# One-hots of four tokens in one comparison, and second-table products one tile behind, in a one-core hybrid layer

## The chip, the cores and the metric

The kernel runs on one core of one Trainium2 chip. The metric is the device time of one execution in microseconds; the median of the runs counts. A separate execution is recorded by the hardware profiler, and all rows below come from that one.

## What is computed

The reference is one layer on x (1024 tokens of 1024 numbers): a token mixer (stick-breaking attention and a gated delta rule), a cross-attention into 256 memory tokens, and a product-key retrieval over 16384 single-neuron experts, each added to x, then a final RMSNorm. What the change touches most is the retrieval:

```python
q = (xt @ w_pq).reshape(T, PEER_HEADS, 2, PEER_QDIM // 2)
s = jnp.einsum('thpd,hpnd->thpn', q, subkeys)
top_s, top_i = lax.top_k(s, PEER_TOPK)
...
best_s, best_pos = lax.top_k(cand_s.reshape(T, PEER_HEADS, kk), PEER_TOPK)
expert = jnp.take_along_axis(cand_i.reshape(T, PEER_HEADS, kk), best_pos, axis=-1)
gate = jax.nn.softmax(best_s, axis=-1)
...
act = jax.nn.gelu(jnp.einsum('thkd,td->thk', peer_u[eb], xb), approximate=False) * gb
return jnp.einsum('thk,thkd->td', act, peer_v[eb])
```

Each token picks 128 experts (8 heads of 16) out of 128 x 128. An expert's row of `peer_u` gives a number, Gelu and the gate weigh it, and it multiplies the expert's row of `peer_v`.

## The kernel before

The program is written with tiles and pools. A planner at build time puts the instructions of each engine in an order: it goes through simulated time with its own durations, and where several instructions are ready for an engine it takes the one that the program emits first. On the chip each engine then runs its list in that order, and semaphores hold it where data or a buffer is missing. So the order in which the Python code emits is a priority, not the order on the chip.

The sequence is done in three groups of tokens (256, 384, 384). Each group goes through `token_mixing`, `cross` and `routing`. In `token_mixing`, `proj` loads 128 columns of a weight at a time, splits them into a high and a low half (`split`: ACT rounds, DVE subtracts), and `mm3` makes three products per 128 rows. The loop at line 468 does this for 1536 columns of the delta rule: each result goes into a tile `c` with three columns of the group before in front (line 471, from `tail`), the last three columns are kept for the next group (line 472), then a short convolution follows (one scaled copy on ACT, three steps on DVE). In `cross`, line 636 divides the exponentials of the softmax by their sum, before PE transposes them.

For retrieval the blocks of 128 tokens are served in two ways. Blocks 0, 1, 2, 3 and 7 are fetched: `fetch` on POOL's queue gathers 128 rows of an expert table by index (line 793, 512 KB), and DVE (lines 809 and 83, or PE in line 838) uses them; the tile `row` has seven buffers, also for other uses. Blocks 4, 5 and 6 (384 tokens) are dense: all 16384 experts are computed, in 128 tiles of 128 experts.

For the dense blocks `choose_t` gives `sel3`: for each token's 128 choices the first key, the second key and the gate, one token in a column. `spread` makes a gate table from it: for each token a one-hot of the first key times the gate (`o0`, DVE, line 913) and a one-hot of the second key (`o1`: for even tokens POOL, line 918; for odd ones ACT, as Relu(1 - |n - key|), lines 915 and 916), each 128x128, in twelve buffers. PE multiplies them (line 919), four tokens into one PSUM tile, ACT copies that into `st` (one buffer), and after eight such groups SP stores `st` in `g_sc` (2 MB). There are 96 groups of four tokens.

The first table's products are in `dense_h`: it loads 128 experts' columns of `peer_ut`, splits them, makes 24 products into a PSUM tile and applies Gelu on ACT. `dense_ahead` does this for the first 36 tiles (`AHEAD`) beside the spreading of blocks 5 and 6: `mix` emits one tile, then 1.83 steps of `pick_gates` (33 steps a block), and so on. `dense` does the other 92 tiles and all products with the second table: for each tile `dense_h` (into the single PSUM tile `hp`), then the load of 128 rows of `peer_v` (`vr`, five buffers), their split (`vh`, `vl`, three buffers), the gating of `h` with `gm` (a part of `g_sc`, loaded for four tiles), the split of that (`ah`, `al`), and 18 products into six PSUM tiles that collect over all tiles. The 36 tiles done ahead come last, with `h` loaded from `h_sc`. The dense steps are emitted in turns with `rest`, the fetching of blocks 2, 3 and 7, of which 320 steps are emitted before.

Of the kernel before, what the change touches and what calls it, by code (L numbers as in the profile page):

```python
# [8 lines left out]
F32 = mybir.dt.float32  # L9
# [11 lines left out]
P = 128  # L21
# [12 lines left out]
ROWS = 7  # L34
WLS = 2
SHS = 3
OBS = 12
ND = 384
TMAX = max(n for _, n in GROUPS)
KD = D // P  # L40
# [11 lines left out]
def block_kernel(ctx: ExitStack, tc: tile.TileContext, x_t, mem_t, gains, cst, sel, eye, w_in, conv, a_log,  # L52
# [23 lines left out]
    def copy(o, i, scale=1.0):  # L76
        return act.activation(o, i, AF.Copy, scale=scale)  # L77

    def func(o, i, f, **kw):
        return act.activation(o, i, f, **kw)  # L80
# [28 lines left out]
    def a_tile():  # L109
        return pa.tile([P, 512], F32, name="acc")  # L110
# [4 lines left out]
    def by4(t):  # L115
        return t.rearrange("p (h t) -> p h t", h=4)
# [334 lines left out]
    def token_mixing(g, t0, T, x1_where, result):  # L451
# [3 lines left out]
        with ExitStack() as eo:  # L455
# [12 lines left out]
            for i, ps in proj(w_in, O_G, 1536, xh, xl, T, share=SH_G):  # L468
                c = po.tile([P, T + 3], F32, name="ev", bufs=2)
                copy(c[:, 3:], ps)  # L470
                vec.tensor_copy(c[:, :3], tail[:, i])
                vec.tensor_copy(tail[:, i], c[:, T:])
                d = qkv[i // 4][:, i % 4]
                copy(d, c[:, 0:T], cv[:, i, 0:1])
                for j in range(1, 4):
                    stt(d, c[:, j:j + T], cv[:, i, j:j + 1], d, OP.mult, OP.add)
# [131 lines left out]
    def cross(g, x1, T):  # L608
        NB = T // P
        with ExitStack() as es:  # L610
            p1 = open_pool(f"c1{g}", 1, where=es)
            tmp = open_pool(f"c2{g}", 2, where=es)
            mK = p1.tile([P, KD, NMEM], F32, name="mK")
            sp.dma_start(mK, mk_sc)
            mV = p1.tile([P, 2, D], F32, name="mV")
            sp.dma_start(mV, mv_sc)
            hi, lo = p1.tile([P, KD, T], F32R, name="xhi"), p1.tile([P, KD, T], F32R, name="xlo")
            norm_t(hi, lo, tmp, lambda k: x1[:, k], 1, T)
            qT = p1.tile([P, KD, T], F32, name="qT")
            for i, ps in proj(w_cq, 0, D, hi, lo, T):  # L620
                copy(qT[:, i], ps, 1.0 / 16)
            oh, ol = p1.tile([P, KD, T], F32R, name="xhi"), p1.tile([P, KD, T], F32R, name="xlo")
            for h in range(4):
                pT = tmp.tile([P, 2, T], F32, name="pT")
                for b in range(NB):
                    bs = slice(b * P, (b + 1) * P)
                    s = z_tile()[:, :NMEM]
                    for k in range(2):
                        pe.matmul(s, lhsT=qT[:, 2 * h + k, bs], rhs=mK[:, 2 * h + k], start=k == 0, stop=k == 1)
                    mx = tmp.tile([P, 2], F32, name="mx")  # L630
                    vec.tensor_reduce(mx[:, 0:1], s, op=OP.max, axis=AX.X)
                    vec.tensor_scalar(mx[:, 0:1], mx[:, 0:1], -1.0, None, op0=OP.mult)
                    p = tmp.tile([P, NMEM], F32, name="p")
                    func(p, s, AF.Exp, bias=mx[:, 0:1], accum_out=mx[:, 1:2])
                    vec.reciprocal(mx[:, 1:2], mx[:, 1:2])
                    vec.tensor_scalar(p, p, mx[:, 1:2], None, op0=OP.mult)
                    tp = a_tile().rearrange("p (m t) -> p m t", m=4)[:, :2]
                    for m in range(2):
                        pe.transpose(tp[:, m], p[:, m * P:(m + 1) * P], ident)
                    copy(pT[:, :, bs], tp)  # L640
                for d in range(2):
                    ps = j_tile()[:, :T]
                    for m in range(2):
                        pe.matmul(ps, lhsT=mV[:, m, (2 * h + d) * P:(2 * h + d + 1) * P], rhs=pT[:, m],
                                  start=m == 0, stop=m == 1)
                    split(oh[:, 2 * h + d], ol[:, 2 * h + d], ps)
            for i, ps in proj(w_co, 0, D, oh, ol, T):
                vec.tensor_add(x1[:, i], ps, x1[:, i])
# [251 lines left out]
    def spread(px_, sel3, b):  # L900


        neg = px_.tile([P, 3, P], F32, name="neg")
        vec.tensor_scalar(neg[:, 0], sel3[:, 1], -1.0, None, op0=OP.mult)
        for c0 in range(0, P, 32):
            st = px_.tile([P, P, 32], F32, name="st")
            for c in range(c0, c0 + 32, 4):
                ps = by4(a_tile())
                for j in range(4):
                    o0 = px_.tile([P, P], F32, name="o0", bufs=OBS)  # L910
                    o1 = px_.tile([P, P], F32, name="o1", bufs=OBS)
                    t = c + j
                    vec.tensor_scalar(o0, io128, sel3[:, 0, t:t + 1], sel3[:, 2, t:t + 1], op0=OP.is_equal, op1=OP.mult)
                    if j % 2:
                        func(o1, io128, AF.Abs, bias=neg[:, 0, t:t + 1])
                        func(o1, o1, AF.Relu, scale=-1.0, bias=1.0)
                    else:
                        pool.tensor_scalar(o1, io128, sel3[:, 1, t:t + 1], None, op0=OP.is_equal)
                    pe.matmul(ps[:, j], lhsT=o1, rhs=o0, start=True, stop=True)
                copy(st[:, :, c - c0:c - c0 + 4], ps.rearrange("p j r -> p r j"))  # L920
                yield
            sp.dma_start(g_sc[(b * P + c0) // 32], st)
# [16 lines left out]
    def dense_h(r, xh, xl, ps, o, eng=vec):  # L939

        raw = wp.tile([P, KD, P], F32, name="raw", bufs=3)
        sp.dma_start(raw, ut_v[:, :, r * P:(r + 1) * P])
        uh = wp.tile([P, KD, P], F32R, name="wh")
        ul = wp.tile([P, KD, P], F32R, name="wl", bufs=WLS)
        split(uh, ul, raw, eng=eng)
        mm3(ps, uh, ul, xh, xl, KD)
        func(o, ps, AF.Gelu)
# [11 lines left out]
    def dense(xh, xl):  # L959
        T = ND  # L960
        NB = T // P
        with ExitStack() as es:
            tmp = open_pool("dv", 2, where=es)
            ps = [f() for f in (z_tile, z_tile, z_tile, a_tile, a_tile, j_tile)][:2 * NB]
            hp = j_tile()[:, :T]
            first = True
            for r0 in [*range(AHEAD, P, RG), *range(0, AHEAD, RG)]:
                gm = tmp.tile([P, T // 32, RG, 32], F32, name="gm")
                sp.dma_start(gm, g_sc[:, :, r0:r0 + RG].rearrange("c p r t -> p c r t"))
                h = tmp.tile([P, RG, T], F32, name="h")  # L970
                if r0 < AHEAD:
                    sp.dma_start(h, h_sc[:, r0:r0 + RG, :T])
                for j in range(RG):
                    r = r0 + j
                    if r0 >= AHEAD:
                        dense_h(r, xh, xl, hp, h[:, j])
                    vr = tmp.tile([P, D], F32, name="vr", bufs=5)
                    sp.dma_start(vr, peer_v[r * P:(r + 1) * P])
                    vh = tmp.tile([P, D], F32R, name="vh", bufs=3)
                    vl = tmp.tile([P, D], F32R, name="vl", bufs=3)  # L980
                    split(vh, vl, vr)
                    hj = h[:, j].rearrange("p (c t) -> p c t", t=32)
                    vec.tensor_mul(hj, hj, gm[:, :, j])
                    ah = tmp.tile([P, T], F32R, name="ah", bufs=3)
                    al = tmp.tile([P, T], F32R, name="al", bufs=3)
                    split(ah, al, h[:, j])
                    for b in range(NB):
                        for a, v in ((ah, vh), (ah, vl), (al, vh)):
                            for d in range(2):
                                pe.matmul(ps[2 * b + d], lhsT=a[:, b * P:(b + 1) * P], rhs=v[:, 512 * d:512 * d + 512],  # L990
                                          start=first and a is ah and v is vh, stop=r == (AHEAD or P) - 1 and a is al)
                    first = False
                    yield
            for b in range(NB):
                blk = order[b]
                rows = slice(blk * P, blk * P + P)
                y = tmp.tile([P, D], F32, name="y")
                sp.dma_start(y, xr_sc[rows])
                for d in range(2):
                    dd = slice(512 * d, 512 * d + 512)  # L1000
                    vec.tensor_add(y[:, dd], ps[2 * b + d], y[:, dd])  # L1001
                last_norm(y, rows)
# [135 lines left out]
```

## Time and profile before

| | us |
|---|---|
| median of 3 runs | 3807.42 |
| lowest, highest | 3803.46, 3813.42 |
| the profiled execution, its own time | 3825.46 |
| its span, first to last instruction | 3823.5 |

Over the span PE is busy 3384.8 us (89%), PE's weight loads 2839.4 (74%), DVE 2848.8 (75%), POOL 1982.3 (52%) and ACT 1614.8 (42%); the DMA engines move 1100.54 MB at a mean of 288 GB/s. These shares are means over stages with different limits. The table by stretch shows each stage by itself: the engine that is busy nearly all of a stretch is the candidate for its limit, and the waits say which engine the others waited for at the end. [...] PEclk is the clock that PE was granted, as a part of full speed.

### The profile page before, as it was taken

Reading aid. Unit: us, or ns where it says so; the run is one execution under the profiler, and the core shown is the slowest. Engines: PE = TensorE matmul, PEld = TensorE weight load, DVE = VectorE, ACT = ScalarE, POOL = GpSimd, SP = SyncE. Lnnn points to the kernel's source line nnn. Section 1 sums busy time; section 2 is a strip of 40 time slices with the busy share of each in tenths; the row PEclk is TensorE's granted clock in tenths of the full one; section 3 lists DMA queues with packets and bytes.
Section 4 is the critical chain, followed back from the end, with each engine's and each line's share of the span. In section 5 each row is a group of like instructions: output and inputs, shape, how many; then the busy total and the mean of one; then the engine's idle time right before and its main releaser. Section 6 shows DMA issues by size and latency. Waiting matters only on the chain. (4 is left out here: it accounts for less than half of the span.)

```text
span 3823.5 us, 57005 instructions
## 1 busy us (share of the span) xinstructions
PE 3384.8 (89%) x20621; PEld 2839.4 (74%) x20621; DVE 2848.8 (75%) x5650; ACT 1614.8 (42%) x2982; POOL 1982.3 (52%) x1611
## 2 busy tenths in 40 slices
PE   7998976999889978999987899999659999999995
PEld 6888866887666755757676677888558888888874
DVE  6445599886566799338987568997767888878886
ACT  5654543664323323545533233565533333343333
POOL 1010007767744456467786455778964444444552
PEclk9999988998989988999978999999779999999998
DMA  6537439997898998999869989989899999999996
GB/s 162 141 91 216 146 107 316 342 310 234 310 358 288 334 327 284 302 318 318 271 219 325 328 288 342 302 294 327 300 323 324 340 344 340 338 325 321 358 385 216
DMA packets 745794, 1100.54 MB, mean 288 GB/s; under 512 B 42148, under 2 KB 554532, under 8 KB 742440
## 3 DMA queue, kind: packets, MB, share of 16 engines
q0 software_dynamic: 184320, 671.17, 49.3%
q1 hardware_dynamic: 561192, 425.73, 36.4%
q8 instruction: 162, 2.65, 0.3%
q14 instruction: 120, 0.98, 0.1%
HBM read 1036.60 MB, written 60.16 MB: 287 GB/s over the span
## 5 line engine op out<-in xcount | busy, mean ns | idle before, releaser
L793 POOL DMA_INDIRECT row<-in_peer_u_dram,ix x640 | 821.9, 1284 | 523.3 <-DVE y L83 152.4
L809 DVE CUSTOM_DVE_ANT_0 row<-row,xs 128x1024 f32<-128x1024 f32 x640 | 827.3, 1302 | 149.3 <-DMA row<-in_peer_u_dram,ix 126.1
L223 PE MATMUL pj<-xhi,wh 128*128 128x384 f32 (+1 forms) x1912 | 640.5, 335 | 58.3 <-ACT xhi L77 21.9
L89 DVE TENSOR_TENSOR wl<-raw,wh 128x1024 fp32r<-128x1024 f32 (+1 forms) x420 | 494.9, 1179 | 252.6 <-ACT wh L77 239.3
L223 PE MATMUL pj<-xhi,wl 128*128 128x384 f32 (+1 forms) x1912 | 641.8, 336 | 33.4 <-POOL wl L89 18.0
L223 PE MATMUL pj<-xlo,wh 128*128 128x384 f32 (+1 forms) x1912 | 626.8, 330 | 11.1 <-DVE xlo L89 11.1
L793 POOL DMA_INDIRECT row<-in_peer_v_dram,it x384 | 442.3, 1152 | 364.2 <-PE ac L838 174.3
L77 ACT ACTIVATE wh<-raw 128x1024 fp32r<-128x1024 f32 (+1 forms) x447 | 449.9, 1007 | 276.0 <-PE pj L223 200.6
L793 POOL DMA_INDIRECT row<-in_peer_v_dram,ix x256 | 341.0, 1332 | 372.7 <-DVE y L83 184.2
L223 PEld LDWEIGHTS pj<-xhi,wh 128*128 128x128 f32 x1912 | 375.4, 196 | 90.9 <-ACT xhi L77 28.2
L223 PE MATMUL pj<-xh,wh 128*128 128x384 f32 x1152 | 400.8, 348 | 46.8 <-ACT h L80 40.9
L223 PEld LDWEIGHTS pj<-xhi,wl 128*128 128x128 f32 x1912 | 375.6, 196 | 71.8 <-POOL wl L89 20.1
L223 PE MATMUL pj<-xh,wl 128*128 128x384 f32 x1152 | 399.1, 346 | 9.7 <-POOL wl L89 5.6
L223 PEld LDWEIGHTS pj<-xlo,wh 128*128 128x128 f32 x1912 | 373.3, 196 | 30.8 <-DVE xlo L89 14.8
L223 PE MATMUL pj<-xl,wh 128*128 128x384 f32 x1152 | 394.1, 343 | 0.3 <-DVE xl L89 0.3
L83 DVE SCALAR_TENSOR_TENSOR y<-row,hh,y 128x1024 f32<-128x1024 f32 x256 | 328.3, 1283 | 8.1 <-DMA row<-in_peer_v_dram,ix 6.6
L838 PE MATMUL ac<-row,sb 128*32 128x256 f32 x3072 | 263.0, 402 | 41.9 <-DMA row<-in_peer_v_dram,it 37.8
L89 POOL TENSOR_TENSOR wl<-raw,wh 128x1024 fp32r<-128x1024 f32 x27 | 65.7, 2433 | 427.4 <-DVE one L773 331.4
L223 PEld LDWEIGHTS pj<-xh,wh 128*128 128x128 f32 x1152 | 221.3, 192 | 68.8 <-ACT h L80 55.4
L77 ACT ACTIVATE vh<-vr 128x1024 fp32r<-128x1024 f32 x128 | 134.9, 1058 | 322.0 <-PE pj L990 301.8
L223 PEld LDWEIGHTS pj<-xh,wl 128*128 128x128 f32 x1152 | 221.4, 192 | 24.7 <-POOL wl L89 7.5
L89 DVE TENSOR_TENSOR vl<-vr,vh 128x1024 fp32r<-128x1024 f32 x128 | 156.6, 1223 | 91.1 <-ACT vh L77 80.7
(453 smaller groups left out, 6514.1 us busy)
## 6 DMA issues: line engine op xcount, KB each, us to landing
raw<-in_w_in_dram SPq DMA_DIRECT2D x132, 512.0 KB
raw<-in_peer_ut_dram SPq DMA_DIRECT2D x128, 512.0 KB
vr<-in_peer_v_dram SPq DMA_DIRECT2D x128, 512.0 KB
raw<-in_w_pq_dram SPq DMA_DIRECT2D x48, 512.0 KB
g_sc<-st SPq DMA_DIRECT2D x12, 2048.0 KB
gm<-g_sc SPq DMA_DIRECT2D x32, 768.0 KB
raw<-in_w_mix_dram SPq DMA_DIRECT2D x24, 512.0 KB
raw<-in_w_cq_dram SPq DMA_DIRECT2D x24, 512.0 KB
```

The costliest lines, as they stand in the source:

```text
L77: return act.activation(o, i, AF.Copy, scale=scale)
L83: return vec.scalar_tensor_tensor(out=o, in0=a, scalar=s, in1=b, op0=op0, op1=op1)
L89: eng.tensor_tensor(lo, src, hi, op=OP.subtract)
L223: pe.matmul(ps, lhsT=a[:, k], rhs=b[:, k], start=i == 0, stop=i == 3 * kt - 1)
L793: pool.indirect_dma_start(out=t, out_offset=None, in_=src, in_offset=bass.IndirectOffsetOnAxis(ap=index, axis=0))
L809: vec.tensor_tensor_reduce(out=t, in0=t, in1=xs, scale=1.0, scalar=0.0, op0=OP.mult, op1=OP.add, accum_out=hh[:, j:j + 1])
L838: pe.matmul(ac[32 * d:32 * d + 32, 256 * w:256 * w + 256], lhsT=sb[:, j], rhs=t[:, 256 * d:256 * d + 256], start=j == 0, stop=j == 31)
```

## The change

There are four edits.

- `spread`: for four tokens one DVE instruction compares the numbers 0 to 127 with both keys of each of the four tokens, into a tile `one` (128 x 2 x 4 x 128, three buffers). The one-hot of the first key is multiplied by the gate on ACT, token by token, in place. POOL's comparison, ACT's Abs and Relu, and the negated keys `neg` are gone. The products are the same.
- `dense`: what a tile needs of the second table is a function `weigh`. It is emitted one tile late: first `dense_h` of tile r+1, then `weigh` of tile r. The last one follows the loop.
- `token_mixing`: the two copies of three columns are made by ACT.
- `cross`: the softmax's scaling is made by ACT.

```diff
-OBS = 12
+OBS = 3
...
-                vec.tensor_copy(c[:, :3], tail[:, i])
-                vec.tensor_copy(tail[:, i], c[:, T:])
+                copy(c[:, :3], tail[:, i])
+                copy(tail[:, i], c[:, T:])
...
-                    vec.tensor_scalar(p, p, mx[:, 1:2], None, op0=OP.mult)
+                    copy(p, p, mx[:, 1:2])
...
-        neg = px_.tile([P, 3, P], F32, name="neg")
-        vec.tensor_scalar(neg[:, 0], sel3[:, 1], -1.0, None, op0=OP.mult)
...
+                one = px_.tile([P, 2, 4, P], F32, name="one", bufs=OBS)
+                vec.tensor_tensor(one, io128[:, None, None, :].to_broadcast([P, 2, 4, P]),
+                                  sel3[:, 0:2, c:c + 4, None].to_broadcast([P, 2, 4, P]), op=OP.is_equal)
                 for j in range(4):
-                    o0 = px_.tile([P, P], F32, name="o0", bufs=OBS)
-                    o1 = px_.tile([P, P], F32, name="o1", bufs=OBS)
-                    t = c + j
-                    vec.tensor_scalar(o0, io128, sel3[:, 0, t:t + 1], sel3[:, 2, t:t + 1], op0=OP.is_equal, op1=OP.mult)
-                    if j % 2:
-                        func(o1, io128, AF.Abs, bias=neg[:, 0, t:t + 1])
-                        func(o1, o1, AF.Relu, scale=-1.0, bias=1.0)
-                    else:
-                        pool.tensor_scalar(o1, io128, sel3[:, 1, t:t + 1], None, op0=OP.is_equal)
-                    pe.matmul(ps[:, j], lhsT=o1, rhs=o0, start=True, stop=True)
+                    copy(one[:, 0, j], one[:, 0, j], sel3[:, 2, c + j:c + j + 1])
+                    pe.matmul(ps[:, j], lhsT=one[:, 1, j], rhs=one[:, 0, j], start=True, stop=True)
...
+            def weigh(r, h, gm):
+                vr = tmp.tile([P, D], F32, name="vr", bufs=5)
+                sp.dma_start(vr, peer_v[r * P:(r + 1) * P])
...
+                split(vh, vl, vr)
+                hj = h.rearrange("p (c t) -> p c t", t=32)
+                vec.tensor_mul(hj, hj, gm)
...
+                split(ah, al, h)
...
+            waiting = None
             for r0 in [*range(AHEAD, P, RG), *range(0, AHEAD, RG)]:
...
                 for j in range(RG):
-                    r = r0 + j
                     if r0 >= AHEAD:
-                        dense_h(r, xh, xl, hp, h[:, j])
...
+                        dense_h(r0 + j, xh, xl, hp, h[:, j])
+                    if waiting:
+                        weigh(*waiting)
+                        yield
+                    waiting = r0 + j, h[:, j], gm[:, :, j]
+            weigh(*waiting)
+            yield
```

## Rows read from the trace of the kernel before

**Rows 1.** By stretch: busy us (x instructions) PE, PEld, DVE, ACT, POOL; clock; DMA; GB/s.
```profile
2418.00:2620.00 202.00, 184.61 (x1200) 163.83 (x1199) 191.52 (x619) 132.63 (x312) 173.10 (x160) 0.92 0.87 297
2620.00:2806.00 186.00, 132.82 (x825) 116.94 (x823) 135.85 (x284) 93.91 (x261) 163.03 (x158) 0.82 0.87 302
2722.00:2806.00 84.00, 38.58 (x179) 34.41 (x177) 65.43 (x131) 34.71 (x104) 76.56 (x72) 0.63 0.74 253
...
2838.00:3594.00 756.00, 725.66 (x3596) 647.60 (x3597) 617.06 (x729) 265.45 (x358) 344.79 (x269) 0.99 1.00 337
3500.00:3600.00 100.00, 97.03 (x483) 86.22 (x481) 91.21 (x89) 33.59 (x46) 59.51 (x44) 1.00 1.06 375
```

**Rows 2.** Waits from 2418 to 2806 us: waiter <- releaser, us, times, longest.
```profile
PEld acc L919 <- POOL o L918: 48.7, 25, 8.8
...
PE acc L919 <- POOL o L918: 42.6, 20, 8.6
```

**Rows 3.** The same view from 2840 to 3780 us.
```profile
POOL row L793 <- DVE y L83: 319.5, 154, 23.9
...
PEld pj L223 <- ACT h L80: 40.2, 42, 3.3
...
PE pj L223 <- ACT h L80: 26.8, 42, 3.0
```

**Rows 4.** Timeline of PE: start, duration in us, what.
```profile
3582.18 0.34 PE L223 MATMUL pj<-xl,wh 128*128 128x384 f32 x1
3583.10 0.44 PE L223 MATMUL pj<-xh,wh 128*128 128x384 f32 x1 [0.58 <-ACT h L80]
3583.38 0.34 PE L223 MATMUL pj<-xh,wl 128*128 128x384 f32 x1
3583.55 0.34 PE L223 MATMUL pj<-xl,wh 128*128 128x384 f32 x1
...
3587.37 0.63 PE L990 MATMUL z<-vh,ah 128*128 128x512 f32 x2
...
3591.49 0.34 PE L223 MATMUL pj<-xh,wh 128*128 128x384 f32 x1
```

**Rows 5.** Groups by line and shape, 2400 to 2840 us: busy, mean ns | idle before.
```profile
L918 POOL TENSOR_SCALAR o<-io,sel 128x128 f32<-128x128 f32 x186 | 164.6, 896 | 13.8 <-PE acc L919 11.7
L913 DVE TENSOR_SCALAR o<-io,sel 128x128 f32<-128x128 f32 x372 | 128.6, 414 | 15.4 <-PE acc L919 15.1
...
L80 ACT ACTIVATE o<-io,neg 128x128 f32<-128x128 f32 x186 | 70.2, 396 | 51.5 <-PE acc L919 47.8 <-PE pj L223 3.3
```

**Rows 6.** By stretch, the one-hots (tile o) alone: PE, PEld, DVE, ACT, POOL.
```profile
2418.00:2620.00 202.00, 58.94 (x392) 53.85 (x392) 70.34 (x196) 57.37 (x196) 83.21 (x94) 0.92 0.87 297
2620.00:2806.00 186.00, 66.14 (x376) 59.66 (x376) 58.22 (x176) 51.03 (x176) 81.36 (x93) 0.82 0.87 302
```

**Rows 7.** Groups of ACT and DVE over the whole run, by shape.
```profile
L77 ACT ACTIVATE vh<-vr 128x1024 fp32r<-128x1024 f32 x128 | 134.9, 1058 | 322.0 <-PE pj L990 301.8 <-DMA raw<-in_peer_ut_dram 20.2
...
L80 ACT ACTIVATE h<-pj 128x384 f32<-128x384 f32 x128 | 62.8, 490 | 235.4 <-PE pj L223 223.2 <-issue 12.1
...
L77 ACT ACTIVATE gc<-ev,cv 128x256 f32<-128x256 f32 x12 | 5.9, 499 | 0.0
...
L834 DVE TENSOR_TENSOR sb<-ey,ht 128x1024 f32<-128x1024 bf16 x12 | 15.3, 1278 | 4.3 <-PE ac L838 4.1 <-issue 0.2
...
L471 DVE COPY ev<-tail 128x3 f32<-128x3 f32 x36 | 13.0, 362 | 0.2
...
L636 DVE TENSOR_SCALAR p<-p,mx 128x256 f32<-128x256 f32 x32 | 11.3, 358 | 1.4
...
L472 DVE COPY tail<-ev 128x3 f32<-128x3 f32 x36 | 8.3, 231 | 14.5 <-ACT ev L77 14.1 <-issue 0.2
```

**Rows 8.** By stretch, the row fetches of line 793 alone: POOL busy (x fetches).
```profile
2418.00:2806.00 388.00, 149.42 (x122) 0.87 0.87 299
2838.00:3786.00 948.00, 435.04 (x329) 0.99 0.98 337
```

More of the change, by code (lines that the diff above doesn't have):

```diff
@@ L965, in dense @@
             hp = j_tile()[:, :T]
-            first = True
+            def weigh(r, h, gm):
+                vr = tmp.tile([P, D], F32, name="vr", bufs=5)
+                sp.dma_start(vr, peer_v[r * P:(r + 1) * P])
+                vh = tmp.tile([P, D], F32R, name="vh", bufs=3)
+                vl = tmp.tile([P, D], F32R, name="vl", bufs=3)
+                split(vh, vl, vr)
+                hj = h.rearrange("p (c t) -> p c t", t=32)
+                vec.tensor_mul(hj, hj, gm)
+                ah = tmp.tile([P, T], F32R, name="ah", bufs=3)
+                al = tmp.tile([P, T], F32R, name="al", bufs=3)
+                split(ah, al, h)
+                for b in range(NB):
+                    for a, v in ((ah, vh), (ah, vl), (al, vh)):
+                        for d in range(2):
+                            pe.matmul(ps[2 * b + d], lhsT=a[:, b * P:(b + 1) * P], rhs=v[:, 512 * d:512 * d + 512],
+                                      start=r == AHEAD and a is ah and v is vh, stop=r == (AHEAD or P) - 1 and a is al)
+            waiting = None
             for r0 in [*range(AHEAD, P, RG), *range(0, AHEAD, RG)]:
@@ L973, in dense @@
                 for j in range(RG):
-                    r = r0 + j
                     if r0 >= AHEAD:
-                        dense_h(r, xh, xl, hp, h[:, j])
[L977 to L993, printed above, removed]
+                        dense_h(r0 + j, xh, xl, hp, h[:, j])
[5 more added lines that the diff above has]
+            yield
             for b in range(NB):
```

## Prediction

> **What bounds the kernel now.** I read the busy time of each engine by stretch first [rows 1], because the edits sit in two stages that have different limits. From 2418 to 2806 us the one-hots of 384 tokens are spread into the gate table (96 groups of four tokens), while `dense_ahead` and the routing's rest run beside them. In the first 202 us DVE is busy 191.5 us (94.8%) and PE 184.6; in the other 186 us POOL has the most, 163.0 us (88%), with DVE at 135.9 and PE at 132.8. The waits of the whole stage then say who ends last: PE and its weight loads wait 42.6 and 48.7 us for POOL's comparison in line 918, by far their largest releaser [rows 2]. The reader is to see a stage bound by DVE first and by POOL after. From 2838 us the dense loop runs, and there PE is busy 725.7 of 756 us at a clock of 0.99 [rows 1]: PE bounds it. DMA is also near full (share 1.00, 337 GB/s), but it isn't what ends PE's waits: those are 42 waits for ACT's Gelu, 26.8 us as PE sees them and 40.2 us as the weight loads do [rows 3]. The timeline shows one: products of the first table end at 3582.18, the next tile's begin at 3583.10 [rows 4]. They need the PSUM tile `hp`, which the Gelu has not yet read. Two tiles of `dense_h` followed each other without the second table's products between them.
>
> **The spread, part by part.** Removed are POOL's comparisons: 186 in the stretch, 896 ns each, 164.6 us of busy time [rows 5]; DVE's gated comparisons, 372 at 414 ns, 128.6 us [rows 5]; ACT's Abs and Relu, two for every second token. One-hots had 58.9 PE, 70.3 DVE, 57.4 ACT and 83.2 POOL us in the first part, and 66.1, 58.2, 51.0 and 81.4 in the second [rows 6]. Added for each group: one DVE comparison that writes 128x1024 numbers, and four ACT scalings of 128x128.
>
> The new DVE comparison has no row. Nearest is the product of line 834, also 128x1024 with a broadcast operand, 1278 ns [rows 7]. Bounds: two of the old 128x128 comparisons, 0.83 us (2 x 414 ns [rows 5]), and four of them, 1.66 us, as it does the work of eight. I take 1.28, the row of the same size. A scaling with a factor per partition has no row at 128x128 either; ACT's Abs with a bias per partition of that size takes 396 ns [rows 5], and I take that, with 0.25 to 0.50 as bounds (the latter is the 128x256 scaling, 499 ns [rows 7]; the former half of it).
>
> First part: DVE 191.5 - 70.3 + 49 groups x 1.28 (62.7) = 183.9 us, and at the present 94.8% this is 194 us, 8 less than 202. Second part: POOL 163.0 - 81.4 = 81.7; DVE 135.9 - 58.2 + 44 x 1.28 (56.3) = 134; ACT 93.9 - 51.0 + 176 x 0.396 (69.7) = 113; PE 132.8 or less, since in the last 84 us it runs at a clock of 0.63 [rows 1]. DVE is then the largest, 134 / 0.948 = 141 us, 45 less than 186. Together 53 us. The lower end is that only the last 84 us gain, where POOL is at 76.6 us and PE at 38.6 [rows 1]: there DVE, with its share of the second part's comparisons (84/186 of 58.2 and of 56.3), would be 65.4 - 26.3 + 25.4 = 64.5, / 0.948 = 68, so 16 us. I take 45, nearer to the upper end because POOL is at 88% through all of the second part, not only at its end. What is late next is DVE, then PE; `st` has a single buffer and waits for its store after every eighth group, before as after.
>
> Each scaling on ACT adds a handover: DVE compares, ACT scales, PE multiplies, ACT empties PSUM. Behind a scaling that waits for DVE stand, on ACT, the Gelu and the weight splits of `dense_ahead`; PE waits for those. Three buffers of four tokens hold as many tokens as twelve of one did, so groups still overlap, and ACT has 94 of 186 us of work now [rows 1]: I cost the handover at nothing. If that cover is gone it is within the gap from 45 to 16.
>
> [...]
>
> **The dense loop.** Emitting `dense_h` of tile r+1 before the products of tile r gives the order first table, second table, first table: the Gelu of one tile (490 ns [rows 7]) then runs beside the other's products, which take 3591.49 - 3587.37 = 4.1 us [rows 4]. Of the gap of 0.92 us, 0.17 is the normal pitch (3583.55 - 3583.38); 42 x 0.75 = 31.5 us, and 36 with the slower first product behind a gap (3583.38 - 3583.10 = 0.28 instead of 0.17) [rows 4]. Below, it is nothing, if another engine paces the loop. DVE's load per tile stays, 617 of 756 us, 85% of 724; DMA would have to move 337 x 756/724 = 352 GB/s. In 3500 to 3600 us DVE is at 91.2%, DMA at 375 GB/s and PE still at 97.0 [rows 1], so both have room. I take 28. The added wait is none: `vh`, `ah` of tile r are ready earlier than PE asks. SP's loads of `vr` move behind the next tile's `raw`; with five and three buffers they are prefetched, at no cost. `gm` (two buffers) is held one tile longer, as its successor is wanted one tile later.
>
> **The small moves.** The two 128x3 copies cost DVE 36 x 362 and 36 x 231 ns, 21.3 us over three groups, [rows 7]; on ACT they have no row, and 72 of them lie between nothing and 28.5 us (396 ns, the 128x128 row [rows 5]); I take half, 14, beside PE's work. ACT no longer waits for DVE before its own scaled copy. I take 2 us gained, 0 to 10. The softmax scaling costs DVE 32 x 358 ns and ACT 32 x 499 [rows 7]: 4.5 us more if all is exposed, hidden if PE's projections cover it; I take 0, from -2 to +8.
> [...]
>
> **What is pushed on.** In the spread stage 122 rows are fetched in 388 us, one in 3.2 us; from 2838 to 3786 it is 329, one in 2.9 us [rows 8]. A stage shorter by 45 us leaves 14 more for later, each 0 to 2.9 us: 0 to 41. I take 5 us, since DVE and DMA have the room named above.
>
> Sum: 45 + 28 + 2 - 5 = 70 us off the profiled execution (span 3823.5, its own time 3825.5), so 3755 there. That execution is 18 us above the median of the runs, 3807.4; I take the same 70 off the median: 3737.
>
> **Rivals.** (a) *The dense gain is missing*: the order of PE comes from a planner that works with its own durations, and it may still run two tiles of the first table in a row, or DVE or DMA paces the loop. Then the change doesn't do there what it says. 45 + 2 - 5: 3765. For it: DMA's share of 1.00; against it: no wait for DMA among PE's.
> (b) *The fetched rows set the end*: with the pace of 2.9 us for a row kept, 45 us taken from the spread give back 41, and the dense loop's 28 come back as 10 rows x 2.9. Time unchanged, 3800 to 3812. For it: POOL waits 319.5 us for DVE's use of the rows [rows 3]. Against it: in 3500 to 3600 us POOL fetched 44 rows (all its instructions there, 2.3 us each) beside a full PE [rows 1].
> (c) *ACT's order turns against PE* (the slower side): `weigh` of tile r stands behind `dense_h` of tile r+1 in the program, so ACT may get the Gelu of r+1 before the split of `vr` of r. The Gelu waits for PE's 24 products, and PE then waits for Gelu and split: 0.490 + 1.058 us [rows 7], for 92 tiles 142 us. Less the spread's 42, 100 us slower: 3907. It decides as soon as it hits more than 27 of the 92 tiles (42 / 1.55). Against it: three buffers of `vh`, and ACT has nothing else to do while PE multiplies, so a planner that takes what is ready would put the split first.
>
> **How the numbers follow.** Forecast (spread and dense both gain) 0.56, (a) 0.22, (b) 0.11, (c) 0.07, and 0.04 for a small loss, 15 to 40 us, from another order of the plan in stages that the edits don't touch. 0.3% of 3807 is 11 us, about what a measurement can tell from no change. Faster is the forecast and (a): 0.78; same is (b) and a part of the small loss: 0.12; slower is (c) and the rest of it: 0.10. The low end has all upper bounds, 53 + 36 + 10 + 2 = 101, so 3706, and 15 more for the plan: 3690. The high end has the lower bounds, 16 + 0 and nothing else, 3791, and goes on to the middle of (b): 3806. Outside stay (c), the small loss and half of (b), under 0.2.
>
> **What would show it.** Right: POOL's share in the spread falls by half and PE's waits for POOL are gone; the one-hots end near 2760 instead of 2806; in the dense loop PE's waits for the Gelu vanish and 100 us hold 12 tiles instead of 11.5 (483 products of 42 a tile [rows 1]); PE's clock stays above 0.63 before the loop. Wrong: the comparison takes well over 1.3 us, ACT is over 90% busy in the spread, DMA waits appear ahead of DVE's row products, or many rows are still fetched after PE has ended.

## The result and the profile after

| | before | after |
|---|---|---|
| median of 6 runs each, us | 3808.49 | 3762.11 |
| lowest, highest | 3803.46, 3821.70 | 3750.96, 3772.83 |
| the profiled execution, its own time | 3825.46 | 3750.96 |
| its span | 3823.5 | 3749.2 |

The ratio is 0.9878 (95% interval 0.9858 to 0.9897): 46 us faster by the medians, and the slowest run of after lies 3803.46 - 3772.83 = 31 us below the fastest of before. The two profiled executions are 74 us apart, because the one of before lies 17 us above its median and the one of after 11 us below.

The table by stretch of the changed kernel (us of the stretch; busy us of PE, PEld, DVE, ACT, POOL with their instructions; clock; DMA share; GB/s), cut at the stores of the gate table: 2441.0 is the first of the twelve stores, 2684.6 the eighth, 2778.2 the last.

```profile
2441.00:2684.00 243.00, 228.77 (x1535) 203.44 (x1534) 224.85 (x461) 174.07 (x383) 137.75 (x90) 0.99 0.96 337
2684.00:2778.00 94.00, 53.33 (x272) 48.85 (x271) 91.84 (x104) 57.68 (x160) 68.42 (x46) 0.73 0.97 362
...
2810.00:3500.00 690.00, 687.76 (x3472) 625.78 (x3472) 569.82 (x670) 249.68 (x343) 348.52 (x237) 1.00 0.99 338
```

The same cut of the kernel before, first to eighth store and eighth to last:

```profile
2447.00:2690.00 243.00, 226.98 (x1513) 204.12 (x1513) 209.33 (x615) 155.14 (x367) 205.69 (x192) 0.94 0.91 313
2690.00:2807.00 117.00, 65.31 (x350) 56.57 (x348) 89.04 (x184) 55.62 (x165) 105.72 (x103) 0.71 0.82 284
```

The reader is to see three things. Two thirds of the spread take 243 us before and after in these two profiles: PE is at 93 to 94% of it in both. The last third went from 117 to 94 us: POOL had 105.7 of 117 (90%), now DVE has 91.8 of 94 (98%). And the dense loop, where PE had 96% [rows 1], is full.

In that last third PE still waits 40 of the 94 us, 38 of them for ACT, which itself waits 46 us for DVE's comparisons in the spread (the row of L77 below):

```profile
PE acc L912 <- ACT st L77: 29.5, 7, 9.9
PE acc L912 <- ACT one L77: 8.6, 12, 1.0
```

The new instructions, 2400 to 2820 us (busy us, mean ns | idle time before):

```profile
L77 ACT ACTIVATE one<-one,sel 128x128 f32<-128x128 f32 x372 | 117.7, 392 | 46.1 <-DVE one L908 46.0
...
L908 DVE TENSOR_TENSOR one<-io,sel 128x1024 f32<-128x1024 f32 x93 | 114.6, 1240 | 7.8 <-PE acc L912 7.7
L912 PEld LDWEIGHTS acc<-one 128*128 128x128 f32 x768 | 110.4, 214 | 61.8 <-ACT st L77 32.9 <-ACT one L77 23.0 <-issue 4.1
```

The comparison takes 1240 ns (1278 was taken), the scaling 392 (396 taken). POOL, which was named most often where the weight loads waited [rows 2], is in that row no more; ACT's copies and scalings are. In the dense loop the waits for the Gelu [rows 3] are gone, but for one of 11 us at its start, ahead of 2810 us, where the kernel before had one of 12 us. From 2810 to 3700 us PE waits 11.8 us in all, and the Gelu waits for PE:

```profile
ACT h L80 <- PE pj L223: 273.3, 87, 5.5
...
PE z L974 <- ACT vh L77: 11.8, 5, 7.3
```

PE's timeline has no gap where [rows 4] had 0.92 us; tiles of the first and second table alternate, one tile in 3402.20 - 3393.92 = 8.28 us:

```profile
3393.74 0.34 PE L223 MATMUL pj<-xl,wh 128*128 128x384 f32 x1
3393.92 0.63 PE L974 MATMUL z<-vh,ah 128*128 128x512 f32 x2
...
3397.81 0.39 PE L974 MATMUL pj<-vh,al 128*128 128x512 f32 x1
3398.04 0.34 PE L223 MATMUL pj<-xh,wh 128*128 128x384 f32 x1
...
3402.02 0.34 PE L223 MATMUL pj<-xl,wh 128*128 128x384 f32 x1
3402.20 0.63 PE L974 MATMUL z<-vh,ah 128*128 128x512 f32 x2
```

The rows fetched between the first and the last store (POOL busy, x fetches, clock, DMA share, GB/s), first after, then before:

```profile
2441.00:2778.00 337.00, 185.05 (x127) 0.92 0.96 344
```

```profile
2447.00:2807.00 360.00, 140.16 (x114) 0.87 0.88 303
```

13 more rows in 23 us less. This goes against the prediction, which let the shorter stage push 14 rows on.

### The profile page after: what moved, and what is told of

Read it like the earlier page. It is cut to its first block, busy times and chain, and to the rows that moved or that the text cites. A ratio compares the mean times of both kernels' runs of the same rounds, so it can differ in the third digit from the quotient of the medians.

```text
span 3749.2 us, 56321 instructions
## 1 busy us (share of the span) xinstructions
PE 3356.5 (90%) x20621; PEld 2821.2 (75%) x20621; DVE 2831.5 (76%) x5255; ACT 1646.3 (44%) x3086; POOL 1848.1 (49%) x1419
## 3 DMA queue, kind: packets, MB, share of 16 engines
q1 hardware_dynamic: 561192, 425.73, 36.9%
q8 instruction: 162, 2.65, 0.3%
## 5 line engine op out<-in xcount | busy, mean ns | idle before, releaser
L793 POOL DMA_INDIRECT row<-in_peer_u_dram,ix x640 | 839.0, 1311 | 546.3 <-DVE hh L809 151.6
L809 DVE CUSTOM_DVE_ANT_0 row<-row,xs 128x1024 f32<-128x1024 f32 x640 | 837.9, 1318 | 124.7 <-DMA row<-in_peer_u_dram,ix 110.5
L77 ACT ACTIVATE wh<-raw 128x1024 fp32r<-128x1024 f32 (+1 forms) x447 | 449.9, 1007 | 277.5 <-PE pj L223 193.9
L793 POOL DMA_INDIRECT row<-in_peer_v_dram,ix x256 | 363.3, 1419 | 379.1 <-DVE y L83 200.2
L77 ACT ACTIVATE vh<-vr 128x1024 fp32r<-128x1024 f32 x128 | 135.0, 1058 | 202.5 <-PE pj L974 202.5
L223 PEld LDWEIGHTS pj<-xl,wh 128*128 128x128 f32 x1152 | 219.2, 190 | 1.5 <-DVE xl L89 0.6
```

Of the source, the lines that this page charges most:

```text
L223: pe.matmul(ps, lhsT=a[:, k], rhs=b[:, k], start=i == 0, stop=i == 3 * kt - 1)
L793: pool.indirect_dma_start(out=t, out_offset=None, in_=src, in_offset=bass.IndirectOffsetOnAxis(ap=index, axis=0))
L809: vec.tensor_tensor_reduce(out=t, in0=t, in1=xs, scale=1.0, scalar=0.0, op0=OP.mult, op1=OP.add, accum_out=hh[:, j:j + 1])
```

## The experiments

The theory after the result: PE's chain and the chain of fetched rows run side by side to the end, and the later one sets it. The spread edit shortens both, the dense edit only PE's. The rivals: two gains that simply add up, or a dense gain that is owed to the rows fetched earlier.

Times of all profiled executions, in us from each trace (loop = first to last Gelu of the dense loop; tail = span minus the end of PE's last product; "rows" = rows fetched by the last store, of 1280 or 1256):

| kernel | median | ratio to before | first, last store | loop | PE's last product | last row product | span | tail | rows |
|---|---|---|---|---|---|---|---|---|---|
| before | 3808.5 | 1 | 2446.7, 2806.7 | 804.5 | 3784.9 | 3814.0 | 3823.5 | 38.6 | 933 |
| before, once more | 3813.2 | 0.9995 | 2430.3, 2792.6 | 804.6 | 3771.6 | 3799.9 | 3809.3 | 37.8 | 934 |
| spread alone | 3804.0 | 0.9976 | 2435.8, 2780.8 | 813.9 | 3763.3 | 3790.8 | 3800.3 | 37.0 | 947 |
| dense alone | 3808.9 | 0.9993 | 2442.8, 2801.6 | 763.3 | 3740.4 | 3801.8 | 3811.3 | 70.9 | 934 |
| small moves alone | 3838.3 | 1.0061 | 2456.3, 2826.3 | 801.4 | 3798.7 | 3827.2 | 3836.6 | 37.9 | 942 |
| spread and dense | 3768.9 | 0.9880 | 2437.6, 2781.3 | 764.3 | 3716.1 | 3757.7 | 3767.1 | 51.1 | 948 |
| after | 3762.1 | 0.9878 | 2441.0, 2778.2 | 763.5 | 3712.3 | 3739.8 | 3749.2 | 36.9 | 964 |
| after, softmax on DVE | 3777.4 | 0.9918 | 2451.7, 2794.5 | 761.5 | 3731.8 | 3766.2 | 3775.6 | 43.9 | 955 |
| before, 24 rows fewer | 3804.1 | 0.9965 | 2433.8, 2795.2 | 801.1 | 3768.2 | 3712.8 | 3792.9 | 24.7 | 933 |
| dense alone, 24 fewer | 3781.3 | 0.9911 | 2430.0, 2787.1 | 762.6 | 3725.3 | 3734.8 | 3764.4 | 39.0 | 934 |
| after, 24 rows fewer | 3755.6 | 0.9848 | 2454.7, 2796.0 | 764.0 | 3730.2 | 3662.0 | 3754.2 | 24.0 | 964 |
| after, two comparisons | 3894.0 | 1.0217 | 2459.9, 2923.1 | 762.7 | 3857.5 | 3886.1 | 3895.5 | 38.1 | 978 |
| after, more on ACT | 3799.8 | 0.9968 | 2459.6, 2828.3 | 764.0 | 3763.3 | 3791.8 | 3801.2 | 37.8 | 974 |
| after, other ring for y | 3754.2 | 0.9856 | 2443.5, 2781.4 | 764.6 | 3717.3 | 3736.4 | 3745.9 | 28.6 | 964 |

The kernel before had a median of 3808 to 3815 us in these comparisons; each ratio is to the runs of its own comparison.

**The edits one by one.** The first is `spread` of the diff alone (with OBS = 3).

> The kernel before with the first edit alone: one comparison for four tokens, gates on ACT. Theory (POOL's comparisons bound the second part of the spread, and the time stays gained): 20 to 45 us below the kernel before by the medians, the last store of the gate table 20 to 30 us earlier, and the dense loop as long as before (804 us from first to last Gelu) with its 40 or so waits of PE for the Gelu. Rival (the fetched rows set the end): the stage is shorter, the dense loop longer by about as much, and the time within 5 us of the kernel before.

9 us (ratio 0.9976, 0.9960 to 0.9991), between theory and rival. The stage from first to last store is 345 us instead of 360 to 362, all of it after the eighth store: 252 us up to there (243 and 247 in the two profiles of before) and 93 behind (117, 116). 13 more rows are fetched by the last store. About 4 us are lost again behind it: from the last store to PE's last product it is 982.5 us, against 978.2 and 979.0 in the two profiles of before. The loop, with its Gelu waits as before, looks 9 us longer because the products of one more tile of the second table fall between its first and its last Gelu (1638 products instead of 1621 in the trace).

The second is `dense` of the diff alone.

```diff
-                        dense_h(r, xh, xl, hp, h[:, j])
-                    (load, split, gating and products of tile r)
+                        dense_h(r0 + j, xh, xl, hp, h[:, j])
+                    if waiting:
+                        weigh(*waiting)
+                    waiting = r0 + j, h[:, j], gm[:, :, j]
```

> The kernel before with the second edit alone: products with the second expert table one tile behind. Theory (PE's waits for the Gelu are the loss, and PE bounds the loop): 28 to 41 us below the kernel before by the medians, the waits for the Gelu gone, the loop 804 us before and 763 to 776 now. Rival (DMA or DVE paces the loop, and the loop's gain in the full change came from the rows that the shorter spread had fetched): the waits for the Gelu go, waits for DMA or DVE come in their place, and the gain is under 15 us.

The ratio is 0.9993 (0.9976 to 1.0009): nothing. But the loop is 763.3 us, 41 shorter, and PE's last product ends 31 and 44 us earlier than in the profiles of before. The theory had the loop and the rival had the time, but not for the rival's reason: from 2840 to 3780 us no group of PE's waits, or of its weight loads', comes to 20 us, and the products of the second table and their weight loads wait for ACT's `vh` alone, 32.4 us in 16 waits. The end of this kernel, by stretch:

```profile
3720.00:3740.00 20.00, 20.00 (x90) 16.52 (x89) 17.78 (x19) 4.99 (x7) 12.31 (x9) 1.00 0.74 226
3740.00:3760.00 20.00, 0.38 (x2) 0.00 (x0) 19.54 (x17) 0.00 (x0) 13.98 (x13) 0.64 0.85 299
3760.00:3780.00 20.00, 0.00 (x0) 0.00 (x0) 16.94 (x14) 8.31 (x12) 11.31 (x11) 0.50 0.96 363
```

PE has nothing from 3740 us on, while POOL issues 24 more row fetches. That is what rival (b) of the prediction forecast, in this kernel alone: the fetched rows took the place of PE's chain. Its pace of 2.9 us for a row isn't kept there, though: DVE makes 25 row products in a run of 33 us.

Third, lines 471, 472 and 636 alone.

> The kernel before with the small moves alone: tail copies and softmax scaling on ACT. Theory (both lie beside PE's work): 0 to 6 us below the kernel before. Rival (the softmax's scaling is exposed on ACT, 141 ns more for each of 32): up to 5 us above it.

25 us slower (ratio 1.0061, 1.0042 to 1.0079), outside both. Its first store is at 2456 us and its stage 370 us long; 833 rows were fetched by the first store instead of 820. From there to the end it takes 3836.6 - 2456.3 = 1380.3 us, as the kernel before does (1376.8 and 1379.0 in its two profiles): the loss arose ahead of the first store.

Fourth, the first two edits without the small moves.

> The kernel before with the first and the second edit and without the small moves. Theory (the gains add up and the small moves carry next to nothing): 40 to 46 us below the kernel before by the medians, as near to the changed kernel (46 below) as the runs can tell. Rival (the small moves matter through another order of the plan): it lies more than 12 us above the changed kernel's 3762.

44 us (0.9880, 0.9859 to 0.9902): as the theory expected, but not by adding up. Alone the two gave 9 and 4 us by the medians, the 4 not clear of nothing; together 44. The rows still end 14 us later than in a kernel where PE sets the end: the tail is 51 us instead of 37.

**Does the profile of before stand for its runs?** The kernel before, unchanged.

> The kernel before once more, for a second profile of it: the first one's execution, 3825.5 us, lay above all other runs. Theory (the 74 us between the first two profiles are some 46 of change and the rest a difference between executions): its own time is near 3808 to 3813, its last matmul near 3768 to 3775 instead of 3785. Rival (profiled executions of this kernel are always that long): 3820 or more again.

The theory holds: 3812 us, and PE's last product at 3771.6. The two executions differ before the spread, 16 us by the first store; from there to the end they take 1376.8 and 1379.0 us. So parts are best compared from the first store on: there the changed kernel takes 3749.2 - 2441.0 = 1308.2, 69 to 71 less, and the kernel with the spread and the dense edit alone 3767.1 - 2437.6 = 1329.5, 47 to 50 less.

**Do the rows hide the dense gain?** Three kernels without the last 24 rows of block 7.

```diff
-        for j in range(NSLOT):
+        for j in range(NSLOT - (24 if blk == 7 else 0)):
             t = fetch(peer_v, ix[:, j:j + 1])
```

> The kernel before without the last 24 fetched rows of block 7 (that part of its sum is left out). Theory (the end is the later of PE's chain and of the fetched rows', and before the change both are within 10 us of each other, PE's tail the later): 0 to 10 us below the kernel before, the last matmul where it was. Rival (the fetched rows alone set the end): 24 rows by 2.5 us, about 55 us below.

> The kernel with the second edit alone, without the last 24 fetched rows of block 7 (left out of its sum). That edit alone ended PE's work 44 us earlier in its profile and gained nothing, with 24 rows fetched after PE's last product. Theory (those rows took its place at the end): without them 25 to 45 us below the kernel before, and the same distance below the kernel before with the same rows left out, less 0 to 10. Rival (the loop's gain is not there, and the profile's early end of PE belongs to one execution): within 12 us of the kernel before.

> The changed kernel without the last 24 fetched rows of block 7 (left out of its sum). Theory (with both edits PE's chain and its tail of 37 us set the end again, the rows being done by then): 0 to 12 us below the changed kernel, 3750 to 3762. Rival (the rows set its end too): 24 rows by 1.3 to 2.5 us, 30 to 55 us below it.

11, 34 and 6 us less (3804.1 against 3815.3; 3781.3 against 3815.3; 3755.6 against 3762.1). The theory holds in all three, within 2 us: the first has 11 where 10 was the most, and the second lies 23 below the first where 24 to 34 was expected. With the dense edit alone, taking the rows away brings the time down by 28 us (3808.9 to 3781.3); in the kernel before and in the changed one by 11 and 6. Those 11 and 6 aren't rows that are late: the planner put the last five row products behind the norms of the dense blocks, and without them the tail is 24 us instead of 37. So PE's chain set the end before, and sets it after; with the dense edit alone the rows did.

**What bounds the spread now?** First the comparison twice.

```diff
                 vec.tensor_tensor(one, ..., op=OP.is_equal)
+                vec.tensor_tensor(one, ..., op=OP.is_equal)
```

> The changed kernel with the comparison of four tokens made twice (the second writes the same numbers). 96 more instructions of 1.24 us, 119 us of DVE. Theory (DVE bounds the spread now, being busy 97 to 99% of it): the stage from the first to the last store of the gate table, 337 us in the changed kernel, grows by 60 to 115 us, less than the 119 only by what row products move out of it, and the end comes 50 to 115 us later. Rival (DVE is full only because row products fill it; PE, ACT or the fetches bound the stage): the row products move into the dense loop, the stage grows by less than 20 us and the end by less than 30.

The stage grew by 126 us (463.3 against 337.3), the end by 132 (3894.0 against 3762.1): above the theory's range, far from the rival. 87 of the 96 added comparisons lie in the stage, and DVE's busy time there rises by 101 us, from 316.7 to 417.6. So all of DVE's added time is on the path, and some more. A full DVE isn't the reason: it is at 94% of the changed kernel's stage and at 90% of this one. PE waits for ACT's scalings, and those for DVE's second comparison:

```profile
PEld acc L914 <- ACT one L77: 119.4, 45, 9.1
PE acc L914 <- ACT one L77: 106.2, 42, 8.7
...
ACT one L77 <- DVE one L910: 89.8, 44, 7.8
```

Then one more pass on ACT, which the expectation reckoned at 75 us:

```diff
                 for j in range(4):
+                    if j < 2:
+                        copy(one[:, 0, j], one[:, 0, j])
                     copy(one[:, 0, j], one[:, 0, j], sel3[:, 2, c + j:c + j + 1])
```

> The changed kernel with one more pass on ACT over the one-hots of two tokens in four, ahead of their scaling (a copy onto itself that changes no number): 192 instructions of 0.39 us, 75 us of ACT, in a stage where ACT is busy 246 of 366 us. Theory (DVE bounds the spread and the handover to ACT costs nothing, as the prediction had it): the stage from the first to the last store of the gate table, 337 to 341 us, grows by 0 to 10 us, the end by no more than 15. Rival (ACT's hop between DVE and PE is on the path in spite of its idle time): the stage grows by 30 to 75 us and the end by as much.

The stage is 368.7 us, 31 longer, the end 38. The rival's lower end, and the theory falls. But the pass isn't 75 us: a copy takes 301 ns and they overlap, 43.8 us of busy time for the 174 in the stage, and ACT's busy time rises only from 231.8 to 264.8 us, by 33. The table of that stage, first to last store, ACT's groups in it, and PE's waits:

```profile
2460.00:2828.00 368.00, 296.94 (x1806) 263.91 (x1805) 331.05 (x579) 264.83 (x715) 225.09 (x144) 0.85 0.94 330
```

```profile
L77 ACT ACTIVATE one<-one,sel 128x128 f32<-128x128 f32 x348 | 112.6, 390 | 0.0
...
L77 ACT ACTIVATE one<-one 128x128 f32<-128x128 f32 x174 | 43.8, 301 | 38.6 <-DVE one L908 38.2
```

```profile
PE acc L914 <- ACT st L77: 33.0, 11, 7.3
PE acc L914 <- ACT one L77: 18.2, 17, 3.2
PE pj L223 <- ACT wh L77: 12.9, 7, 5.2
```

ACT is busy 72% and DVE 90%, and still nearly all of ACT's added time is on the path: 31 us of the stage for 33 us of ACT. As PE sees it, the waits for ACT rose from 44.6 to 65.0 us, all waits from 54.4 to 70.4, and its 1806 products take 296.9 us instead of 282.1, at a granted clock of 0.85 instead of 0.92 over the stage. So the chain of comparison, scaling and product paces the spread now, not one full engine.

**Which of the small moves?** The changed kernel with line 636 back on DVE.

> The changed kernel with the softmax's scaling back on DVE (the tail copies stay on ACT). In the profiles at hand the small moves put the last store of the third group's residual about 12 us later (2356, 2370 and 2380 us with them, 2350 to 2366 without). Theory (the softmax's scaling is what is exposed, ACT being slower at it): 5 to 12 us below the changed kernel's 3762, and that store near 2357 or before. Rival (the tail copies or the order of the plan do it, or it is the difference between executions): within 5 us of 3762, and that store still between 2356 and 2380.

15 us slower than the changed kernel (3777.4), against both. The third group's last store of the residual is at 2373 us, as late as with both moves, so the softmax's scaling isn't what makes the stages ahead longer. What differs is again the rows: 829 fetched by the first store instead of 838. By the profiles 16 us arise behind the first store (1323.9 us to the end instead of 1308.2): 5 in the stage and 7 in the tail, which is 44 us again, as where the rows set the end.

**A shorter tail.** The residual of the three dense blocks in the ring of `vr`.

```diff
-                y = tmp.tile([P, D], F32, name="y")
+                y = tmp.tile([P, D], F32, name="vr", bufs=5)
                 sp.dma_start(y, xr_sc[rows])
```

> The changed kernel with the residual of the dense blocks loaded into the ring of five buffers that the second table's rows used, in place of a ring of two: after PE's last product the third block's residual was loaded only once the first block was done (its addition began 3726.4 us, PE's last product ended 3712.3). Theory (that load is on the path to the end): 8 to 14 us below the changed kernel's 3762. Rival (the last five fetched rows end then anyway): within 4 us of it.

3754.2 us, 8 below the changed kernel, and the tail 28.6 instead of 36.9 us, as expected. In the changed kernel the chain that ended last held that load, with the third block's addition behind it:

```profile
3720.92 5.32 DMA y<-xr_sc
3726.36 1.30 DVE y L1000 x2
```

With the other ring the additions of the dense blocks are made right behind PE's last product, and what is late next is the load of the norm's gains into a `row` buffer:

```profile
3714.36 0.26 DVE vr L1000
...
3722.86 5.68 DMA row<-in_g_final_dram
```

This is the fastest kernel here, though its 8 us are close to what the runs can tell: they lie from 3747.7 to 3756.7 us, those of the changed kernel from 3751.0 to 3772.8.

## Why the prediction was right and wrong

The sign was right, and the time, 3762, lies in the range; the likeliest value, 3737, was 25 us too low. From the first store to the end the change takes 69 to 71 us, as many as the sum of 70, and that is luck: the spread gave half of what was forecast, the dense loop half as much again, and 21 us came with the small moves, 6 of them in the spread; 2 were forecast for them.

**The spread: 45 forecast, 23 to 25 measured** (stage 337.3 against 360.0 and 362.3), of which 15 to 19 are the edit's own: the two kernels with it and without the small moves have 345.0 and 343.7. The step that failed is "I take 45, nearer to the upper end because POOL is at 88% through all of the second part". That part is a mean over two limits. From 2620 us to the eighth store PE was full, at a clock of 1.00:

```profile
2620.00:2690.00 70.00, 67.58 (x477) 60.37 (x476) 46.81 (x102) 38.89 (x99) 58.01 (x57) 1.00 0.96 333
```

PE's waits for POOL's comparison in the kernel before, from the first store to the eighth (2447 to 2690 us):

```profile
PE acc L919 <- POOL o L918: 0.4, 1, 0.4
```

and from there to the last (2690 to 2807 us):

```profile
PE acc L919 <- POOL o L918: 41.5, 18, 8.6
```

Up to the eighth store there was nothing for POOL's relief to give. The 8 us of the first part did not come either: DVE lost one-hot work there, but PE, at 91% in the same row of [rows 1], was as near its limit. In the 243 us from the first to the eighth store DVE now has 224.9 us instead of 209.3, and PE 93 to 94%. The lower bound, that only the last stretch gains, was the right reading: behind the eighth store, 117 us in place of the 84 that the prediction cut, it is 22 to 24 us instead of 16. In that stretch POOL gave way to DVE as forecast. The step that counted on 122 rows as fixed failed too: row products of lines 809 and 83 between the stores rose from 75 to 95, 93.5 to 126.1 us of DVE, so what POOL's relief freed was filled with rows.

**The handover, "I cost the handover at nothing".** Wrong. 33 us more of ACT's busy time made the stage 31 us longer while ACT had over a quarter of it idle. What the handover of the change itself costs wasn't measured alone.

**The comparison.** 1240 ns as a mean, where 1278 was taken, inside the bounds of 0.83 and 1.66 us. The median of all 96 comparisons is 1216 ns.

**The dense loop: 28 forecast, 41 measured** (804.5 to 763.5, and 763.3 to 764.3 in the two other kernels of the table with this edit and all their rows). The mechanism was right, the size off: 42 waits were counted in the window, but 44 times in the whole loop of before a Gelu starts 5.0 us behind the one ahead, as two tiles of the first table in a row do. The slower first product behind the gap, kept out of the value taken, belongs to it, and one of the waits is 3.0 us [rows 3] instead of 0.58 [rows 4]: 44 x (0.75 + 0.11) + 2.4 = 40.2. Neither DMA nor DVE paced PE: from 2810 to 3700 us its 11.8 us of waits are all for ACT's `vh`, and its weight loads wait 13.8 us for that and 0.3 for DVE. So rival (a) falls.

**Rows pushed on: 5 lost forecast, rows gained.** The step "a stage shorter by 45 us leaves 14 more for later" took the pace of 3.2 us a row as fixed [rows 8]. POOL issues the fetches, its comparisons stood ahead of them, and without these the pace between the stores is 337/127 = 2.65 us; with the spread edit alone it is 345/122 = 2.8. By the last store the changed kernel has fetched 964 rows, before 933, and 18 of those 31 were ahead by the first store already. 31 fewer are left for a loop that takes one in 2.9 us [rows 8]; that is room of 90 us on the rows' chain, an estimate from these rows. Without it the dense gain would have been lost, as the dense edit alone shows. So rival (b) was no alternative to the forecast: it is what each edit's gain depends on.

**Rival (c)**, ACT's order, did not come: PE waits five times, 11.8 us, for `vh` from 2810 to 3700 us.

**The small moves: 2 forecast.** Alone 25 us slower; on top of the other two 7 us faster by the medians, which the runs can hardly tell (3751.0 to 3772.8 us with them, 3763.2 to 3774.0 without). The step that failed is the price put on them by their durations: ACT's tail copies take 199 ns each and its softmax scaling 504 instead of 358, 14 and 5 us in all. Ahead of the spread they cost more. The third group's last store of the residual comes at 2380 us with them, against 2356 to 2363 in the three other kernels of that comparison, and at 2370 against 2351 to 2355 in the kernels of the next: 15 to 24 us later, by one profile of each. Behind the first store they cost nothing alone (1380.3 us to the end) and give 21 us on top of the other two edits (1308.2 against 1329.5): 6 in the stage and 14 in the tail, where the rows set the end. With both moves 833 and 838 rows were fetched by the first store, without them 819 to 825. That store is later too: 2441, 2444, 2455 and 2456 us in four kernels with both moves (without the two that load the spread itself), 2430 to 2447 in seven without. My reading is that the planner fills the freed DVE time with row products, which delays PE's path ahead of the spread and relieves the rows' chain: a loss where PE sets the end, a gain where the rows do. That is argued from these counts; it wasn't shown by a kernel that holds the rows back. Nor do the two durations of the scaling tell what its move is worth: ACT takes 504 ns for one where DVE takes 358, and yet with the scaling back on DVE the kernel is 15 us slower.

**The same 70 off the median.** The profiled execution was forecast at 3755 and is 3751; for the median the sum missed by 25. This step made it: the profile of before lies 17 us above its median, and the profile of the changed kernel 11 below. Both differences show ahead of the spread. The first store of before came at 2446.7 us, against 2430.3 in the second profile. The changed kernel's last store of the residual came at 2356 us, against 2361 to 2380 in the five other kernels with both moves. Against the second execution of before the change takes 60 us off (3809.3 to 3749.2), and by the medians 46. What of the rest belongs to the small moves and what to the spread between executions stays open.

**The signs named in advance.** POOL's share of the spread fell from 86% (311.4 of 360 us) to 61% (206.2 of 337), not by half; the last store is at 2778 us, where the one-hots were to end near 2760; PE's waits for POOL's comparison are gone, and those for the Gelu but for one of 11 us at the loop's start; the loop's 91 steps from Gelu to Gelu take 763.5 us, 11.9 tiles in 100 us against 11.3 before (804.5); the clock in the last 94 us is 0.73. None of the wrong signs came: ACT is busy 231.8 of 337 us (69%) in the spread, DVE's row products wait 0.7 us for a DMA there (20 before), and three rows are fetched after PE has ended.

## What to carry over

Where two chains run side by side to the end, price each edit on both, and take the later one: here one edit gave 9 us, the other nothing clear, and both together 44. Cut a stretch where the waits change, not in the middle: a mean of 88% for POOL hid 70 us in which PE was full. An engine that issues transfers and also computes has a second price, the transfers that stand behind its work; count them as a pace that the edit changes, not as fixed: here one row in 360/114 = 3.2 us became one in 2.65. An engine with idle time wasn't free here, between two others: 33 us more on ACT, which was then busy 72% of the stage, cost 31. And compare two profiles from a common mark, the part ahead of it by itself, before a difference of spans is carried to a median.

## What the runs showed of the hardware

Two executions of the same program came to the first store of the gate table at 2430.3 and 2446.7 us, and then took 1379.0 and 1376.8 us to the end: nearly all of their difference arose ahead of it.

Beside the dense loop, with the DMA share at 0.98, one row is fetched every 2.9 us [rows 8]. In the kernel with the dense edit alone, after PE had ended, DVE used one row in 11.85 / 9 = 1.32 us, with little between one and the next (one such product there takes 1.28 us by the median):

```profile
3751.20 11.85 DVE L83 SCALAR_TENSOR_TENSOR y<-row,hh,y 128x1024 f32<-128x1024 f32 x9
```

From the issue of a fetch to the use of its row it was 6.8 us there, against 19 to 23 us for the rows that the kernel before fetched from 3700 to 3753 us, beside PE's last products. That is about what seven buffers at 2.9 us a row make, 20 us, an estimate. In these two kernels a row fetched behind PE's end, at 1.32 us, was thus cheaper than one beside its products, at 2.9.
